# The second gate's weights move behind the first expert's, and the router works on the residual's own sums

## The chip, the cores and the metric

One core of a Trainium2 chip runs the whole kernel. The metric is device time in microseconds (us), as the median over runs. The profile is one further execution of the same program, taken by the hardware profiler.

## The reference, cut to what matters

One transformer block on 256 tokens of width 1024, all in 32-bit floats. `cond @ w_ada` gives six rows of 1024: a shift, a scale and a gate for the mixer, and the same three for the expert layer. The mixer's output `y` enters a residual, which is normalised; the router then picks 4 of 32 experts for each token.

```
shift1, scale1, gate1, shift2, scale2, gate2 = split(cond @ w_ada + b_ada)
y = hybrid_mixer(x * (1 + scale1) + shift1)        # attention, gated linear attention, pooling, @ w_out
x = layer_norm(ALPHA * x + (1 + gate1) * y)
h = x * (1 + scale2) + shift2
logits = h @ w_router + b_router                   # top 4 of 32 for each token, softmax over the 4
y = sum over a token's experts of gate * (clamped_swiglu(h @ w_gate_up[e] + b) @ w_down[e] + b_down[e])
x = layer_norm(ALPHA * x + (1 + gate2) * y)
```

The weights of the 32 experts are read once each: 8 MB for `w_gate_up[e]` and 4 MB for `w_down[e]`.

## The kernel before, in words

The tokens are two tiles of 128 (`t` = 0, 1), the width is eight columns of 128 (`k` = 0 to 7). Work runs in two stages: the block up to the routing, and the expert loop.

**The weight ring.** Nearly all weights pass through tiles of 2 MB (tag `w`, `ring_tile`, line 122), filled by DMAs issued on SyncE's queue (SP) in one fixed order. In the first stage five slots exist (`NA`). The expert stage opens a second pool of three (`NB`), in the memory of the first stage's `early` pool; from there on eight slots are used in turn, five loads into the first pool and three into the second. A load is issued when its slot is free, and SP stands still on a load whose slot is not. The order before: input projection, shift and scale columns, `w_out` (`wo`), the router's weights (`wr`), the gate of the mixer (`ada_g1`, two tiles), the gate of the experts (`ada_g2`, two tiles), then the jobs of the experts: four tiles `g0_0` to `g0_3` (the first expert's gate and up weights), four of expert 1, two of expert 0's down weights, and so on (lines 758 and after).

**The first stage's end.** After the attention, VectorE (DVE) sums the two gates over eight products of a tile row with `cond` (lines 620 to 624): `acc` for the first gate, which TensorE (PE) adds up over partitions into `g1p`, and `g2p` for the second. PE multiplies with `wo` (`py`). For each `t`, DVE forms the residual in place (lines 661, 662: `yg`, `y`), its statistics, and the normalised `n1`. PE turns `n1` (`ph`), DVE and ACT apply `hA` and `hB` column by column into `h2T` (lines 680, 682), PE multiplies with the router's weights (`plg`), a bias is added (`lgp`) and PE turns the result back into rows (`plt`, `lg`). Top 4, one-hots, and a count of earlier tokens follow (`top`, `oh`, `msel`, `ppos`, `posm`): `posm` is the place of a token among its expert's rows.

**The expert loop.** Experts go in pairs. `dispatch` (line 776) makes one-hot rows `pp` from `posm` and gathers the pair's tokens by matmuls of `n1` with `pp` (`pxg`), then applies `hA` and `hB` (`xg`). `gate_up` multiplies `xg` with four tiles of weights, so that a quarter of it frees one slot; `down` follows one expert later. Ahead of pair 6 a branch for overfull experts stands (`more_slots`), with a barrier; until there SP may load only the eight tiles behind the pair's end.

The order on each engine is not the program's: the framework lays it out when the program is built, by priority (earlier in the program first) and by its own model of durations. In the run, each engine follows that order.

Of the kernel before, what the change touches and what calls it, by code (L numbers as in the profile page):

```python
# [9 lines left out]
F32 = mybir.dt.float32  # L10
# [4 lines left out]
OP = mybir.AluOpType  # L15
# [97 lines left out]
def block_kernel(ctx: ExitStack, tc, x, w_ada, w_in, gla_w_a2, pool_w, w_out, w_router, w_gate_up, b_gate_up,  # L113
# [48 lines left out]

    half = const.tile([P, 8], F32, name="half")
# [7 lines left out]
    def layer_norm_stats(st, pool, name):  # L171
        mv = pool.tile([P, 2], F32, tag=f"mv{name}", name=f"mv{name}")
        V.bn_aggr(mv, st.rearrange("p a b -> p (a b)"))
        rs = pool.tile([P, 1], F32, tag=f"rs{name}", name=f"rs{name}")
        rsqrt(rs, mv[:, 1:2], 1.0, LN_EPS, 1, pool, f"rt{name}")
        return mv[:, 0:1], rs


    with tc.tile_pool(name="early", bufs=1) as ea, tc.tile_pool(name="late", bufs=1, side="right") as la_, \
# [30 lines left out]
        def load_cols(j, nm):  # L210
            ts = []
            for i in range(2):
                t = ring_tile(f"{nm}_{i}").rearrange("p (k n) -> p k n", n=D)
                SY.dma_start(t, w_ada[0, i * 512:(i + 1) * 512, j * D:(j + 1) * D].rearrange("(k p) n -> p k n", p=P))
                ts.append(t)
            return ts
# [35 lines left out]
        wr = la_.tile([P, KT, NE], F32, name="wr")  # L252

# [10 lines left out]
        ada_m.append(load_cols(4, "adam1"))  # L264
        wo = {}
# [103 lines left out]
        z2 = la_.tile([P, TT, ZN - O_GV], F32, name="z2")  # L369
# [10 lines left out]
        z_gv = z2[:, :, 0:GVW]  # L380
        z_gr = z2[:, :, GVW:]
# [16 lines left out]
        def second_part(n):  # L398

            c0, c1 = ((W1, W2), (W2, C_GA))[n]  # L400
            for t in range(TT):
                b = bank(f"pz2{t}{n}", "z")
                for k in range(KT):
                    mm(b[:, :c1 - c0], hT[:, k, t * P:(t + 1) * P], wz2[n][:, k], k == 0, k == KT - 1)
                if n == 0:
                    o = C_GV - W1
                    V.tensor_add(z1[:, t, O_GA - o:O_GA], b[:, :o], zb[:, O_GA - o:O_GA])
                    V.tensor_add(z2[:, t, 0:GVW], b[:, o:c1 - c0], zb[:, O_GV:O_GR])
                else:
                    V.tensor_add(z2[:, t, GVW:], b[:, :c1 - c0], zb[:, O_GR:ZN])  # L410
# [3 lines left out]
        gaT = ea.tile([RANK, S], F32, name="gaT")  # L414
# [127 lines left out]
        for j in range(2):  # L542
            acc = la_.tile([P, D], F32, tag=("acc", "g1p")[j], name=f"accm{j}")
            A.mul(acc, ada_m[j][0][:, 0], cond[:, 0:1])
            for k in range(1, KT):
                V.scalar_tensor_tensor(acc, ada_m[j][k // 4][:, k % 4], cond[:, k:k + 1], acc, op0=OP.mult, op1=OP.add)
# [45 lines left out]
        o_gla = la_.tile([P, TT, GVW], F32, name="o_gla")  # L592
# [26 lines left out]

        g1p = la_.tile([P, D], F32, tag="g1p", name="g1p")  # L620
        for ts, acc in ((ada_g1, la_.tile([P, D], F32, tag="acc", name="acc1")), (ada_g2, g2p)):
            V.tensor_scalar(acc, ts[0][:, 0], cond[:, 0:1], None, op0=OP.mult)
            for k in range(1, KT):
                V.scalar_tensor_tensor(acc, ts[k // 4][:, k % 4], cond[:, k:k + 1], acc, op0=OP.mult, op1=OP.add)
            if acc is not g2p:
                for n in range(2):
                    b = bank(f"pg1{n}")
                    mm(b, ones, acc[:, n * 512:(n + 1) * 512], True, False)
                    add_row(b, R_G1 + n, 512, False)
                    V.tensor_scalar(g1p[:, n * 512:(n + 1) * 512], b, 1.0, None, op0=OP.add)  # L630
# [13 lines left out]
        lgp = la_.tile([P, S], F32, tag="qin", name="lgp")  # L644
# [8 lines left out]
        oh = []  # L653
        for t in range(TT):
# [12 lines left out]
            A.activation(n1[:, t, 0:512], xs[:, t, 0:512], AF.Identity, bias=nmr, scale=rs)  # L667
# [3 lines left out]
            for q in range(2):  # L671
                b = bank(f"ph{t}{q}").rearrange("p (j s) -> p j s", j=4)
                for j in range(4):
                    k = 4 * q + j
                    T.transpose(b[:, j], twos(n1[:, t], k), ident)
                for j in range(4):
                    k = 4 * q + j
                    o = h2T[:, k, t * P:(t + 1) * P]
                    if j % 2:
                        A.activation(o, b[:, j], AF.Identity, bias=hB[:, k:k + 1], scale=hA[:, k:k + 1])  # L680
                    else:
                        V.tensor_scalar(o, b[:, j], hA[:, k:k + 1], hB[:, k:k + 1], op0=OP.mult, op1=OP.add)
            b = bank(f"plg{t}")
            for k in range(KT):
                g = slice(32 * (k // 2), 32 * (k // 2) + 32)
                mm(b[g, :P], wr[:, k], h2T[:, k, t * P:(t + 1) * P], k % 2 == 0, k % 2 == 1)
            V.tensor_scalar(lgp[:, t * P:(t + 1) * P], b[:, :P], colv[:, 80:81], None, op0=OP.add)
            b = bank(f"plt{t}")
            mm(b[:, 0:NE], lgp[:, t * P:(t + 1) * P], kc[:, K_I4:K_I4 + NE], True, True)
            V.tensor_copy(lg[:, t], b[:, 0:NE])  # L690
# [11 lines left out]
            V.scalar_tensor_tensor(posm[:, t], b[:, 0:NE], 1.0, msel[:, t], op0=OP.add, op1=OP.mult)  # L702

# [71 lines left out]

    def dispatch(pcol, gcol, nm):
# [3 lines left out]
        for t in range(TT):  # L780
            V.tensor_tensor(pp[:, t], pcol[:, t, :, None].to_broadcast([P, 2, CAP]),
                            iota1[:, None, :].to_broadcast([P, 2, CAP]), op=OP.is_equal)
        xg = wk.tile([P, KT, P], F32, tag="xg", name=f"xg{nm}")
        bs = [mps.tile([P, 4, P], F32, tag="m", name=f"pxg{nm}_{q}") for q in range(2)]
        for t in range(TT):
            for k in range(KT):
                mm(bs[k // 4][:, k % 4], twos(n1[:, t], k), pp[:, t].rearrange("p a s -> p (a s)"),
                   t == 0 and k % 4 == 0, t == TT - 1)
        for k in range(KT):
            if k % 2:  # L790
                A.activation(xg[:, k], bs[k // 4][:, k % 4], AF.Identity, bias=hB[:, k:k + 1], scale=hA[:, k:k + 1])  # L791
            else:
                V.tensor_scalar(xg[:, k], bs[k // 4][:, k % 4], hA[:, k:k + 1], hB[:, k:k + 1], op0=OP.mult, op1=OP.add)  # L793
# [157 lines left out]
    for e in range(NE):  # L951
        i, m = divmod(e, 2)
        if m == 0:
            if i == PAIR_MORE:
                finish_down()
                while done[0] < 12 * i + NA + NB:
                    load_next()
# [8 lines left out]
        if e == 0:  # L966
            last_scale()
            V.tensor_mul(bdn, bdn, g2p[0:NE])
# [59 lines left out]
    r = [wk.tile([P, D], F32, tag="xg", name=f"r{t}") for t in range(TT)]  # L1028
# [42 lines left out]
```

## Time and profile before

| | |
|---|---|
| median of 3 runs | 1128.66 us (1127.93 to 1134.68) |
| profiled execution | 1129.8 us, span 1128.0 us |
| PE busy | 1035.4 us, 92% of the span |
| DVE busy | 318.7 us, 28% |
| bytes moved | 449.49 MB, 398 GB/s over the span |
| DMA queue of SP | 95.7% of 16 engines' span |

The span is the profiled execution's own; 1.8 us lie around it. The granted clock of TensorE is told as a share of full speed: 1.00 is 2.4 GHz, 0.50 is 1.2 GHz. A busy share is an average over stages: the gaps that matter are found by looking at stretches of the span.

### The profile page before, as it was taken

To read this page: it belongs to the slowest core of one execution; us is meant where nothing else is said; L and a number is where in the kernel's file an instruction comes from. 1 tells how busy PE (TensorE), PEld (TensorE's weight loads), DVE (VectorE), ACT (ScalarE), POOL (GpSimd) and SP (SyncE) were. 2 spreads that over 40 slices of the span, in tenths; PEclk is the share of its full clock that TensorE was granted. 3 is DMA by queue.
4 is the path that set the end of the run, shared out by engine and by line. 5 is a ranking of instruction groups with operands and counts; after the bars stand their busy time and mean duration, and the time that the engine had idled before them with its cause. 6 is when DMAs were issued, how large, how long until landed. Compare 5 with 4: busy or idle time off the path is not lost.

```text
span 1128.0 us, 11046 instructions
## 1 busy us (share of the span) xinstructions
PE 1035.4 (92%) x4734; PEld 436.9 (39%) x4735; DVE 318.7 (28%) x587; ACT 98.8 (9%) x205; POOL 41.5 (4%) x43
## 2 busy tenths in 40 slices
PE   6999998999999999996999999989989898989795
PEld 3656545434333333333344343423333333333231
DVE  1459694322222122211122221213221121211113
ACT  1024112100000000000000000000000000000100
POOL 2270000000000000000000000000000000000000
PEclk9999897999999999998999999999999999999998
DMA  9997499999999999999899999999999999999992
GB/s 324 348 385 283 181 378 373 428 423 428 428 428 427 428 428 428 428 427 423 344 427 428 428 428 426 428 427 428 428 428 427 428 429 427 428 427 428 428 414 92
DMA packets 52998, 449.49 MB, mean 398 GB/s; under 512 B 5056, under 2 KB 18768, under 8 KB 28496
## 3 DMA queue, kind: packets, MB, share of 16 engines
q1 hardware_dynamic: 52320, 447.90, 95.7%
q8 instruction: 39, 0.64, 0.2%
q10 hardware_dynamic: 624, 0.83, 0.2%
q14 instruction: 15, 0.12, 0.0%
HBM read 447.67 MB, written 1.05 MB: 398 GB/s over the span
## 4 chain that ended last, share of the span: by engine, by line
PE 29%; DMA 22%; DVE 1%; issue 1%; ACT 0%; POOL 0%; DVEq 0%; POOLq 0%
DMA d<-in_w_down 22%; PE gu L134 13%; PE py L134 7%; PE pxg L134 4%; PE ya L134 3%; PE pyl L134 1%; PE paT L837 1%; DVE yb L855 0%; DVE aT L839 0%; DVE res L919 0%; ACT n L931 0%; PE pln L134 0%; DVE r L1038 0%; DVE yl L1015 0%; DVE st L1019 0%
## 5 line engine op out<-in xcount | busy, mean ns | idle before, releaser
L134 PE MATMUL gu<-g,xg 128*64 128x512 f32 x2048 | 462.5, 595 | 14.0 <-DMA g<-in_w_gate_up 12.6
L134 PEld LDWEIGHTS gu<-g,xg 128*64 128x64 f32 x2048 | 143.2, 137 | 295.5 <-issue 261.0
L134 PE MATMUL py<-d,aT 128*64 128x512 f32 x992 | 227.1, 600 | 13.8 <-DMA d<-in_w_down 12.5
L825 DVE TENSOR_SCALAR g<-gu 128x512 f32<-128x512 f32 x32 | 22.1, 692 | 410.1 <-PE gu L134 410.1
L134 PEld LDWEIGHTS py<-d,aT 128*64 128x64 f32 x992 | 70.0, 137 | 150.5 <-issue 140.8
L134 PE MATMUL pxg<-pp,n 128*128 128x128 f32 x512 | 77.0, 302 | 14.9 <-DVE aT L839 7.0
L134 PEld LDWEIGHTS pxg<-pp,n 128*128 128x128 f32 x512 | 69.2, 208 | 43.0 <-issue 29.6
L855 DVE TENSOR_TENSOR yb<-py,g2p 64x512 f32<-64x512 f32 x60 | 41.3, 689 | 139.0 <-PE py L134 138.4
L134 PE MATMUL ya<-yb,sg_None 128*128 128x512 f32 x120 | 58.2, 607 | 4.9 <-DVE yb L855 4.8
L829 ACT ACTIVATE s<-g 128x512 f32<-128x512 f32 x32 | 20.2, 630 | 464.4 <-DVE g L825 464.4
L793 DVE TENSOR_SCALAR xg<-pxg,hA,hB 128x128 f32<-128x128 f32 x64 | 25.8, 409 | 99.2 <-PE pxg L134 90.0
L791 ACT ACTIVATE xg<-pxg,hB,hA 128x128 f32<-128x128 f32 x64 | 28.7, 457 | 274.3 <-DVE xg L793 273.6
L134 PE MATMUL pz<-wz,hT 128*128 128x512 f32 (+2 forms) x128 | 52.4, 547 | 0.0
L169 POOL TENSOR_TENSOR rsb<-rtb,half 128x2 f32<-128x2 f32 x1 | 0.7, 701 | 950.9 <-DVE rtb L168 950.9
L839 DVE COPY aT<-paT 128x512 f32<-128x512 f32 x32 | 22.1, 692 | 43.9 <-PE paT L837 43.8
L134 PE MATMUL py<-wo,oT 128*128 128x512 f32 x64 | 30.9, 629 | 0.2 <-ACT oT L642 0.2
L134 PEld LDWEIGHTS ya<-yb,sg_None 128*128 128x128 f32 x120 | 20.4, 189 | 26.9 <-issue 17.4
L134 PEld LDWEIGHTS pz<-wz,hT 128*128 128x128 f32 x128 | 23.4, 190 | 17.3 <-issue 14.3
L837 PEld LDWEIGHTS paT<-kc,l 128*128 128x128 f32 x128 | 18.0, 209 | 25.3 <-DVE l L831 15.4
L837 PE MATMUL paT<-kc,l 128*128 128x128 f32 x128 | 23.7, 308 | 0.0
L831 DVE TENSOR_TENSOR l<-l,s 128x512 f32<-128x512 f32 x32 | 22.1, 691 | 3.4 <-DVE l L830 0.5
L134 PE MATMUL pqk<-hT,wz 128*128 128x256 f32 x96 | 22.2, 381 | 0.7 <-DVE hT L332 0.7
(245 smaller groups left out, 519.1 us busy)
## 6 DMA issues: line engine op xcount, KB each, us to landing
g<-in_w_gate_up SPq DMA_DIRECT2D x128, 2048.0 KB, 30.4
d<-in_w_down SPq DMA_DIRECT2D x62, 2048.0 KB, 30.4
adam<-in_w_ada SPq DMA_DIRECT2D x4, 2048.0 KB, 16.7
adag<-in_w_ada SPq DMA_DIRECT2D x4, 2048.0 KB, 9.0
ada<-in_w_ada SPq DMA_DIRECT2D x6, 1024.0 KB, 11.1
wz<-in_w_in SPq DMA_DIRECT2D x8, 760.0 KB, 9.5
wo<-in_w_out SPq DMA_DIRECT2D x2, 1536.0 KB, 10.0
ada<-in_w_ada SPq DMA_DIRECT2D x4, 512.0 KB, 7.4
```

The source lines that it names most:

```text
L134: T.matmul(o, l, r, start=start, stop=stop, skip_group_check=True, **kw)
L169: G.tensor_tensor(o, t[:, :n], half[:, :n], op=OP.pow)
L791: A.activation(xg[:, k], bs[k // 4][:, k % 4], AF.Identity, bias=hB[:, k:k + 1], scale=hA[:, k:k + 1])
L793: V.tensor_scalar(xg[:, k], bs[k // 4][:, k % 4], hA[:, k:k + 1], hB[:, k:k + 1], op0=OP.mult, op1=OP.add)
L825: V.tensor_scalar(g, gu[:, 0], LIMIT, None, op0=OP.min)
L829: A.activation(s, g, AF.Sigmoid, scale=SW_ALPHA)
L831: V.tensor_mul(l, l, s)
L837: T.transpose(b[:, j], act[:, j::4], ident)
L839: V.tensor_copy(aT, b)
L855: V.tensor_mul(yb[m * CAP:(m + 1) * CAP, n * 512:(n + 1) * 512], b[r], g2p[r, n * 512:(n + 1) * 512])
```

## The change

Four things are done, and the tiles are laid out anew to make room.

1. The two tiles of the second gate (`adag2`) leave the first stage. They become jobs 4 and 5 of the expert stage, behind `g0_0` to `g0_3`; DVE sums them after the first expert's `gate_up`, and `last_scale` goes to expert 1. The ring's turn is shifted: of eight loads, numbers 3, 4 and 5 now go to the second pool, so `g0_3` and the two `adag2` tiles lie there.
2. The first gate's tiles are loaded ahead of `wo`, `wr` behind the small constants, and the first gate's sum stands ahead of the linear attention's output.
3. The router works on the residual's sums: `wr2` is the router's weights times `hA` (and times `hB`), their column sums give two rows `rrow` (made behind the attention), and the logits are `rs * (y @ wr2) + rs*(-mu) * row 0 + row 1`. So PE turns `y` itself, as each half is ready, and ACT copies four columns at once.
4. The first pair's tokens are gathered in the routing loop, one `t` at a time, into a tile `xgA` of the outer pool (`gathered`, `modulated`), with its one-hots in `g2p`'s memory. `xgA` then serves the even pairs, one tile of the inner pool the odd.

```
-            i = int(turn[0] % (NA + NB) >= NA)
+            i = int(3 <= turn[0] % (NA + NB) < 3 + NB)
...
+    def one_hot(pp, pcol, t):
+        V.tensor_tensor(pp[:, t], pcol[:, t, :, None].to_broadcast([P, 2, CAP]),
+                        iota1[:, None, :].to_broadcast([P, 2, CAP]), op=OP.is_equal)
+    def gathered(bs, pp, t):
+        for k in range(KT):
+            mm(bs[k // 4][:, k % 4], twos(n1[:, t], k), pp[:, t].rearrange("p a s -> p (a s)"),
+               t == 0 and k % 4 == 0, t == TT - 1)
+    def modulated(xg, bs):
+        for k in range(KT):
+            if k % 2:
+                A.activation(xg[:, k], bs[k // 4][:, k % 4], AF.Identity, bias=hB[:, k:k + 1], scale=hA[:, k:k + 1])
+            else:
+                V.tensor_scalar(xg[:, k], bs[k // 4][:, k % 4], hA[:, k:k + 1], hB[:, k:k + 1], op0=OP.mult, op1=OP.add)
+    def summed(acc, ts):
+        A.mul(acc, ts[0], cond[:, 0:1])
+        for k in range(1, KT):
+            V.scalar_tensor_tensor(acc, ts[k], cond[:, k:k + 1], acc, op0=OP.mult, op1=OP.add)
...
         ada_m.append(load_cols(4, "adam1"))
+        ada_g1 = load_cols(2, "adag1")
         wo = {}
...
-        SY.dma_start(wr.rearrange("p (i k) n -> p i k n", k=2), w_router[0].rearrange("(i p k) n -> p i k n", p=P, k=2))
-        ada_g1 = load_cols(2, "adag1")
-        ada_g2 = load_cols(5, "adag2")
...
+        acc1 = la_.tile([P, D], F32, tag="acc", name="acc1")
+        summed(acc1, ada_g1)
...
+        wr2 = la_.tile([P, 2, KT, NE], F32, tag="qin", name="wr2")
+        for j, h in enumerate((hA, hB)):
+            V.tensor_mul(wr2[:, j], wr, h[:, :, None].to_broadcast([P, KT, NE]))
+        wrs = la_.tile([P, 2, NE], F32, name="wrs")
+        V.tensor_reduce(wrs, wr2.rearrange("p j k e -> p j e k"), axis=AX.X, op=OP.add)
+        b = bank("prow")
+        mm(b[:, 0:2 * NE], ones, wrs.rearrange("p j e -> p (j e)"), True, False)
+        mm(b[:, NE:2 * NE], colv[:, 80:81].to_broadcast([P, P]), kc[:, K_I4:K_I4 + NE], False, True)
+        rrow = la_.tile([P, 2, NE], F32, name="rrow")
+        V.tensor_copy(rrow, b[:, 0:2 * NE].rearrange("p (j e) -> p j e", j=2))
...
                 V.bn_stats(st6[:, n], y)
+                b = bank(f"ph{t}{n}").rearrange("p (j s) -> p j s", j=4)
+                for j in range(4):
+                    T.transpose(b[:, j], twos(xs[:, t], 4 * n + j), ident)
+                A.copy(h2T[:, 4 * n:4 * n + 4, t * P:(t + 1) * P], b)
...
+            row = la_.tile([P, NE], F32, tag="row", name=f"row{t}")
+            V.scalar_tensor_tensor(row, rrow[:, 0], nmr, rrow[:, 1], op0=OP.mult, op1=OP.add)
+            b = bank(f"plg{t}")
+            for k in range(KT):
+                mm(b[:, 0:NE], h2T[:, k, t * P:(t + 1) * P], wr2[:, 0, k], k == 0, k == KT - 1)
+            V.scalar_tensor_tensor(lg[:, t], b[:, 0:NE], rs, row, op0=OP.mult, op1=OP.add)
...
             V.scalar_tensor_tensor(posm[:, t], b[:, 0:NE], 1.0, msel[:, t], op0=OP.add, op1=OP.mult)
+            one_hot(ppA, posm[:, :, 0:2], t)
+            if t == 0:
+                first = [bank(f"pxgA{q}", "z").rearrange("p (j s) -> p j s", j=4) for q in range(2)]
+            gathered(first, ppA, t)
+        modulated(xgA, first)
...
+        if e == 0:
+            jobs += [("gate", 0, lambda e, i: load_columns(5, i, f"adag2_{i}"), (0, i)) for i in range(2)]
...
-                while done[0] < 12 * i + NA + NB:
+                while done[0] < 12 * i + 2 + NA + NB:
...
         if e == 0:
+            summed(g2p, weights("gate", 0))
+        elif e == 1:
             last_scale()
```

## Rows read from the trace of the kernel before

**Rows 1.** The page: rate in 40 slices; SP's queue; the chain's lines.

```profile
GB/s 324 348 385 283 181 378 373 428 423 428 428 428 427 428 428 428 428 427 423 344 427 428 428 428 426 428 427 428 428 428 427 428 429 427 428 427 428 428 414 92
...
q1 hardware_dynamic: 52320, 447.90, 95.7%
...
DMA d<-in_w_down 22%; PE gu L134 13%; PE py L134 7%; PE pxg L134 4%; PE ya L134 3%; PE pyl L134 1%; PE paT L837 1%; DVE yb L855 0%; DVE aT L839 0%; DVE res L919 0%; ACT n L931 0%; PE pln L134 0%; DVE r L1038 0%; DVE yl L1015 0%; DVE st L1019 0%
```

**Rows 2.** Stretches: length, busy by engine, then PE's clock, DMA share, GB/s.

```profile
126.00:141.00 15.00, 14.97 (x75) 8.91 (x75) 9.47 (x15) 0.98 (x2) 2.66 (x2) 0.96 0.01 4
147.00:186.00 39.00, 33.43 (x132) 20.01 (x132) 30.72 (x78) 8.09 (x17) 1.10 (x2) 0.82 0.98 399
186.00:191.00 5.00, 5.00 (x29) 2.44 (x30) 1.95 (x6) 3.00 (x5) 0.00 (x0) 1.00 0.70 290
191.00:200.00 9.00, 9.00 (x46) 3.10 (x44) 0.00 (x0) 0.00 (x0) 0.00 (x0) 1.00 0.91 353
200.00:505.00 305.00, 294.99 (x1382) 113.94 (x1378) 67.67 (x118) 18.83 (x38) 0.00 (x0) 1.00 1.01 427
...
580.00:1000.00 420.00, 389.73 (x1822) 148.75 (x1818) 89.35 (x163) 24.50 (x50) 0.00 (x0) 1.00 1.01 427
```

**Rows 3.** Timeline of SP's queue: start, length, line, operation, count.

```profile
117.98 0.37 SPq L214 DMA_DIRECT2D adag<-in_w_ada  x1
140.13 0.37 SPq L214 DMA_DIRECT2D adag<-in_w_ada  x1
147.09 0.34 SPq L737 DMA_DIRECT2D g<-in_w_gate_up  x1
164.54 1.03 SPq L737 DMA_DIRECT2D g<-in_w_gate_up  x2
190.91 3.76 SPq L742 DMA_DIRECT2D d<-in_w_down  x2
```

**Rows 4.** Waits of SP's queue in its first 200 us: total, times, longest.

```profile
SPq L742 <- PE gu L134: 27.3, 2, 24.3
```

**Rows 5.** Timeline of PE: start, length, line, operation, output and inputs.

```profile
119.09 2.48 PE L134 MATMUL pcol<-kc,accm 128*128 128x4 f32 x16
...
153.94 10.57 PE L134 MATMUL py<-wo,oT 128*128 128x512 f32 x24 [0.24 <-ACT oT L642]
165.17 1.22 PE L675 MATMUL ph<-kc,n 128*128 128x128 f32 x8 [0.67 <-ACT n L667]
...
181.59 5.69 PE L134 MATMUL pxg<-pp,n 128*128 128x128 f32 x32
...
187.21 7.09 PE L134 MATMUL gu<-g,xg 128*64 128x512 f32 x32
...
220.10 4.04 PE L134 MATMUL pxg<-pp,n 128*128 128x128 f32 x32
```

**Rows 6.** Timeline of DVE and ACT: sums, linear attention's state, residual, routing, one copy.

```profile
116.68 1.28 DVE L546 SCALAR_TENSOR_TENSOR accm<-adam,cond,accm 128x1024 f32<-128x1024 f32 x1
124.47 0.36 DVE L588 COPY sts<-kv 128x192 f32<-128x192 f32 x1 [1.32 <-PE kv L134]
164.64 0.68 DVE L661 TENSOR_TENSOR yg<-py,g1p 128x512 f32<-128x512 f32 x1
165.36 0.69 DVE L662 SCALAR_TENSOR_TENSOR n<-n,yg 128x512 f32<-128x512 f32 x1
178.24 0.19 DVE L690 COPY lg<-plt 128x32 f32<-128x32 f32 x1 [0.73 <-PE plt L134]
180.62 0.19 DVE L702 SCALAR_TENSOR_TENSOR posm<-ppos,msel 128x32 f32<-128x32 f32 x1 [0.26 <-PE ppos L134]
202.38 0.63 ACT L829 ACTIVATE s<-g 128x512 f32<-128x512 f32 x1 [11.91 <-DVE g L825]
```

**Rows 7.** Timeline around the barrier: PE's last down product, SP's next load.

```profile
510.29 3.65 PE L134 MATMUL py<-d,aT 128*64 128x512 f32 x16 [1.16 <-DMA d<-in_w_down]
550.65 0.82 SPq L742 DMA_DIRECT2D d<-in_w_down  x2
```

More of the change, by code (lines that the diff above doesn't have):

```diff
@@ L161, in add_row @@
         mm(o, sel[:, r:r + 1].to_broadcast([96, P]), row3[:, :n], start, True)
+    xgA = const.tile([P, KT, P], F32, name="xgA")
     half = const.tile([P, 8], F32, name="half")
@@ L176, in layer_norm_stats, with load_columns @@
         return mv[:, 0:1], rs
+    def one_hot(pp, pcol, t):
[15 more added lines that the diff above has]
+            V.scalar_tensor_tensor(acc, ts[k], cond[:, k:k + 1], acc, op0=OP.mult, op1=OP.add)
+    def load_columns(j, i, name):
+        t = ring_tile(name).rearrange("p (k n) -> p k n", n=D)
+        SY.dma_start(t, w_ada[0, i * 512:(i + 1) * 512, j * D:(j + 1) * D].rearrange("(k p) n -> p k n", p=P))
+        return [t[:, k] for k in range(4)]
     with tc.tile_pool(name="early", bufs=1) as ea, tc.tile_pool(name="late", bufs=1, side="right") as la_, \
@@ L210, in load_cols @@
         def load_cols(j, nm):
[L211 to L216, printed above, removed]
+            return load_columns(j, 0, f"{nm}_0") + load_columns(j, 1, f"{nm}_1")
         first_ada = load_ada1(0)
@@ L368, in block_kernel @@
         z1 = ea.tile([P, TT, O_GV], F32, name="z1")
-        z2 = la_.tile([P, TT, ZN - O_GV], F32, name="z2")
+        z_gv = la_.tile([P, TT, GVW], F32, name="z_gv")
+        z_gr = la_.tile([P, TT, GVW], F32, tag="gr", name="z_gr")
         a = W1 - C_FV
@@ L407, in second_part @@
                     V.tensor_add(z1[:, t, O_GA - o:O_GA], b[:, :o], zb[:, O_GA - o:O_GA])
-                    V.tensor_add(z2[:, t, 0:GVW], b[:, o:c1 - c0], zb[:, O_GV:O_GR])
+                    V.tensor_add(z_gv[:, t], b[:, o:c1 - c0], zb[:, O_GV:O_GR])
                 else:
-                    V.tensor_add(z2[:, t, GVW:], b[:, :c1 - c0], zb[:, O_GR:ZN])
+                    V.tensor_add(z_gr[:, t], b[:, :c1 - c0], zb[:, O_GR:ZN])
         lin = ea.tile([P, TT, FH + GKW], F32, name="lin")
-        gaT = ea.tile([RANK, S], F32, name="gaT")
+        gaT = ea.tile([P, 2, S], F32, tag="pm", name="gaT")[0:RANK, 0]
         b = bank("gaT")
@@ L543, in block_kernel @@
             acc = la_.tile([P, D], F32, tag=("acc", "g1p")[j], name=f"accm{j}")
-            A.mul(acc, ada_m[j][0][:, 0], cond[:, 0:1])
-            for k in range(1, KT):
-                V.scalar_tensor_tensor(acc, ada_m[j][k // 4][:, k % 4], cond[:, k:k + 1], acc, op0=OP.mult, op1=OP.add)
+            summed(acc, ada_m[j])
             b = bank(f"pcol{j}", "z")[:, 0:32].rearrange("p (q m) -> p q m", q=8)
@@ L591, in block_kernel @@
                                            op0=OP.mult, op1=OP.add)
-        o_gla = la_.tile([P, TT, GVW], F32, name="o_gla")
+        acc1 = la_.tile([P, D], F32, tag="acc", name="acc1")
+        summed(acc1, ada_g1)
+        o_gla = la_.tile([P, TT, GVW], F32, tag="gr", name="o_gla")
         for t in range(TT):
@@ L617, in block_kernel @@
             V.tensor_mul(o_gla[:, t], o_gla[:, t], sg[:, t])
-        g1p = la_.tile([P, D], F32, tag="g1p", name="g1p")
[L621 to L630, printed above, removed]
+        wr2 = la_.tile([P, 2, KT, NE], F32, tag="qin", name="wr2")
[8 more added lines that the diff above has]
+        V.tensor_copy(rrow, b[:, 0:2 * NE].rearrange("p (j e) -> p j e", j=2))
+        g1p = la_.tile([P, D], F32, tag="g1p", name="g1p")
+        for n in range(2):
+            b = bank(f"pg1{n}")
+            mm(b, ones, acc1[:, n * 512:(n + 1) * 512], True, False)
+            add_row(b, R_G1 + n, 512, False)
+            V.tensor_scalar(g1p[:, n * 512:(n + 1) * 512], b, 1.0, None, op0=OP.add)
         py = [[bank(f"py{t}{n}", "z") for n in range(2)] for t in (1, 0)][::-1]
@@ L653, in block_kernel @@
         oh = []
+        ppA = g2p[:, 0:TT * P].rearrange("p (t m s) -> p t m s", t=TT, m=2)
         for t in range(TT):
@@ L774, in weights @@
         return loaded.pop((kind, e))
+    evens = [str(i) for i in range(0, NE // 2, 2)]
     def dispatch(pcol, gcol, nm):
@@ L780, in dispatch @@
         for t in range(TT):
[L781 to L793, printed above, removed]
+            one_hot(pp, pcol, t)
+        if nm == "0":
+            xg = xgA
+        else:
+            xg = xgA if nm in evens else wk.tile([P, KT, P], F32, tag="xg", name=f"xg{nm}", bufs=1)
+            bs = [mps.tile([P, 4, P], F32, tag="m", name=f"pxg{nm}_{q}") for q in range(2)]
+            for t in range(TT):
+                gathered(bs, pp, t)
+            modulated(xg, bs)
         def gates(m=None):
@@ L1027, in block_kernel @@
     stats = [(mv[:, t, 0:1], rs[:, t:t + 1]) for t in range(TT)]
-    r = [wk.tile([P, D], F32, tag="xg", name=f"r{t}") for t in range(TT)]
+    r = [xgA.rearrange("p k s -> p (k s)"), wk.tile([P, D], F32, tag="xg", name="r1", bufs=1)]
     for t in range(TT):
```

24 lines of the change are left out of this document (1 added, 23 removed).

## The prediction

> **What bounds the kernel now.** I read the page's rate by slices first, then its chain, then stretches, then SP's queue. The rate stands at 427 to 428 GB/s in nearly every slice from the eighth on, and the chain that ends last is mostly DMA of down weights [rows 1]: the expert loop is bound by the stream of weights. From 200 to 505 us and from 580 to 1000 us the stream runs at 427 GB/s without a hole [rows 2]. So the kernel ends a fixed time after the stream starts for good, and only holes in the stream, or bytes still to come, can move it.
>
> The reader should see the holes before 200 us. From 126 to 141 us nothing flows (4 GB/s), though PE is busy throughout [rows 2]: SP stands at the fourth gate tile until 140.13, because its slot is freed only when DVE has half summed the first gate [rows 3]. After that everything goes out that eight slots can hold: `g0` and `g1`, the last of them just behind 164.54 [rows 3]. SP then waits up to 24.3 us for `gu`, PE's first expert product [rows 4]: all eight slots are full, and nothing can be loaded until a quarter of `gu` has been computed. `gu` starts at 187.21 [rows 5], the next load goes out at 190.91 [rows 3], 3.7 us later. The stream sags to 290 GB/s from 186 to 191 and recovers [rows 2]. **That instant, 190.91, is what counts**: the hole at 126 costs nothing by itself, as slots are full well before.
>
> **The balance of the change.** Before, when the slots are full they hold eight tiles of experts 0 and 1, and the second gate is already used up. After, they hold `g0`, the two gate tiles and only two tiles of expert 1. So when the stream starts for good, two more tiles of 2 MB (2.097 million bytes) are still to come: at 427 GB/s [rows 2] 4.91 us each, **9.8 us lost**. What is gained is how much sooner `gu` starts. Break-even is `gu` at 187.21 - 9.8 = 177.4.
>
> A rule bears on this price. The Trainium skill (DMA: Bandwidth & Descriptors, Where 436 GB/s comes from) says that the memory side, about 358 GB/s for a core, binds such loads. By that the two tiles would cost 11.7 us (an estimate) and the sum would come out 1.9 us later; the trace's 427 GB/s disagrees, and decides.
>
> **When `gu` starts, step by step.**
>
> *Up to the last `py`.* PE is busy nearly without a break from 126 (14.97 of 15 us to 141 [rows 2]) to 164.5, where the last `py` ends (153.94 + 10.57) [rows 5], so taking 20 us of gate sums off DVE doesn't end it sooner: the gate's rows for PE (`pg`) only move forward among the same work. What is put in front of it now: the residual's transposes, 12 of 16 ahead of the last half (8 took 1.22 us [rows 5], so 1.8); logits of `t` = 0, 16 passes at the pace of the small products that also load 128 columns each (2.48/16 = 0.155 [rows 5]; 1.9 to 2.5, I take 1.9, since those ran with stalls); the two row products, 0.4. The last `py` ends at 164.5 + 4.1 = **168.6**. Lower bound 164.5 if all of it falls into gaps; upper 171.5 if sums of the first gate, 1.28 us each [rows 6], get in front of links of the linear attention's state on DVE, of which the row at 124.47 is one [rows 6]: two or three such collisions, 2.6 to 3.8 us, that PE's other work can't hide.
>
> *Residual to logits.* `yg` and `y` take 164.5 to 166.05 before [rows 6]: 1.55 us, so 170.15. Behind it four transposes (0.6), ACT's copy of 128x512, priced by another ACT pass of that size (0.63 [rows 6]; from PSUM rather than SBUF, so 0.5 to 0.9), the last eight passes of the logits (1.0), `lg` (0.2), and 0.3 of handovers: 2.7. In PE's order the gather of `t` = 0 may stand in front of these transposes; I count 0.7 of its 2 to 2.85 us. `lg` ends at **173.6**. The statistics run beside: five small operations after `y`, at the 0.2 to 0.7 of such rows [rows 6], so 1 to 3.5 us, and 3.2 are there.
>
> *Logits to place.* From `lg`'s end (178.43) to `posm`'s (180.81) it is 2.4 us [rows 6], and nothing in it changes: 176.0. One-hot 0.3: 176.3.
>
> *Gather of `t` = 1.* Half of `pxg`. The whole took 5.69 us here and 4.04 us at 220 [rows 5]; halves 2.85 and 2.0. The clock granted is 0.82 over 147 to 186 and 1.00 at 200 to 505 [rows 2]; I take 2.4. **`gu` starts at 178.7**, since its first columns of `xg` are ready before the gather ends. The Trainium skill (TensorE: Matmul & The Clock Gate, Part 1) has the clock low by default and released by activity. By that the fuller PE queue favours 2.0, and the sum would be 0.4 us less; the rows at both levels agree in sense.
>
> *First load and end.* 178.7 + 3.7 = 182.4. Against 190.91 that is 8.5 us gained; less 9.8: **1.3 us later**.
>
> **Edits at nothing.** The first gate's loads take `wo`'s early slots and `wo` theirs; the same bytes flow, and SP is at the loads behind them by 117.98 [rows 3], with `py` starting behind `pcol`, which ends at 121.6 [rows 5]. If a part of `wo` came late, PE would wait for one tile of the stream, up to 4.9 us; the 3.6 us between the two rows cover most of it. `wr` goes ahead of the second part's weights; it is 0.13 MB, 0.3 us at 427 GB/s, and that is its cost if a stage waits for them. The two `adag2` tiles and `g1_0`, `g1_1` queue on SP behind slots of the second pool, free when the linear attention's output is done, ahead of the `py` row at 153.94 [rows 5]; `wo`'s second slot comes free last, at 168.6, and one tile of 4.9 us is in before 182. Without that cover: second rival. The second gate's sum (one ACT pass, seven of 1.28 us) runs on DVE while PE does two halves of `gu` of 7.09 us [rows 5], and its slots come back before the stream needs them. `last_scale` moves by one expert and stays ahead of the first `down`. In the loop the alternating `xg` tiles are two as before. At the barrier PE waits 1.16 us for the last down tile [rows 7], so the data already set that point; the hole before 550.65 [rows 7] stays.
>
> The profiled execution was 1129.8 us, 1.1 above the median of 1128.66. So 1131.1 by its count, 1130.0 by the median's.
>
> **Rivals.**
>
> *Routing shortens in full* (faster, but little). All small work hides, `py` ends at 164.5, nothing stands in front of the transposes: `gu` at 173.5, 5.2 us earlier: 1125. For it: DVE is nearly free of sums from 130 on. Against: PE follows an order laid out before the run, and earlier work has priority over the last `py`.
>
> *Slots of the second pool come late* (slower). The new layout puts `adag2` into memory that a tile of the routing holds to its end, about 176. SP, in order, stands in front of four tiles, 19.6 us of stream, which then start at 176 and make expert loads follow at 195.6, where break-even is 181.1: 14.5 later, 1143. It decides as soon as that slot is freed after 161.5. Against: before, the three loads of that pool left right behind 164.54, long ahead of `posm` [rows 3, 6].
>
> *Routing doesn't get shorter.* PE's order puts work of `t` = 0 that waits on DVE ahead of `t` = 1, and `gu` stays between 183 and 187: 1134.5 to 1138.5. For it: PE's queue already stood waiting in this stretch, 5.6 us idle of 39 [rows 2].
>
> *The filled hole pays by itself.* If more slots than eight took part, or the stream never stopped, some 15 us of 126 to 141 would come back: 1115. Against: SP's 24.3 us wait [rows 4].
>
> **How the numbers follow.** Forecast 0.55 (1127 to 1133.5), full shortening 0.18, no shortening 0.16, late slots 0.06, filled hole 0.05. The range 1124 to 1138 holds the first three; own range of the likeliest 1127 to 1133.5. A measurement tells about 1%, 11.3 us, from no change: faster by that only in the last case, slower in the late slots and a tail of no shortening. Faster 0.05, same 0.87, slower 0.08.
>
> **What would show it.** SP: `g0` issued from about 118 on, no hole of 15 us, then a longer one before the restart; restart near 182. PE: `gu` at 177 to 181, the last `py` at 167 to 170. Stream 427 GB/s from there. I am wrong if `gu` starts before 172 or after 187, if the restart doesn't follow `gu` by 3.7 us, or if the time doesn't move by restart plus 9.8.

## The result: 8.4 us slower, and the profile after

The changed kernel takes 1136.68 us (median of 12 runs, 1133.29 to 1139.76) against 1128.30 for the kernel before on the same chip (12 runs, 1126.05 to 1134.68): ratio 1.0058, 95% interval 1.0039 to 1.0077. That is slower beyond its interval, though inside the 1% called "no change" beforehand. The time lies in the stated range of 1124 to 1138, but the likeliest case said 1130 (1127 to 1133.5) and was missed. What came are the numbers of the third rival, "routing doesn't get shorter": `gu` between 183 and 187, 1134.5 to 1138.5. Its reason holds only in part, as the step by step account shows.

The page of the kernel after: rate in 40 slices, chain by line. They answer to [rows 1].

```profile
GB/s 319 351 380 257 279 370 186 430 427 427 429 427 426 429 427 427 427 428 425 353 428 430 427 426 428 427 429 427 428 429 426 427 429 426 427 429 427 427 416 108
...
DMA d<-in_w_down 22%; PE gu L134 9%; PE py L134 6%; DMA g<-in_w_gate_up 4%; PE ya L134 3%; PE pxg L134 3%; PE pyl L134 1%; PE paT L865 1%; DVE aT L867 0%; DVE yb L883 0%; DVE res L947 0%; DVE yl L1045 0%; DVE xgA L1068 0%; DVE st L1049 0%; DVE xgA L1062 0%
```

The bound is the same: from the eighth slice on the stream runs at 425 to 430 GB/s, but for the same dip in the twentieth and the last two slices. So the difference has to lie ahead of that. The fifth slice rose from 181 to 279, the seventh fell from 373 to 186.

Stretches of the kernel after, columns as in [rows 2]: length, busy time by engine, then PE's clock, DMA share, GB/s.

```profile
126.00:141.00 15.00, 15.00 (x51) 8.65 (x52) 10.53 (x17) 0.49 (x1) 1.03 (x1) 0.78 0.52 196
147.00:186.00 39.00, 36.24 (x153) 22.61 (x154) 20.49 (x66) 7.85 (x15) 2.04 (x3) 0.93 0.72 289
186.00:191.00 5.00, 5.00 (x24) 1.61 (x22) 5.00 (x10) 1.68 (x4) 0.00 (x0) 0.89 0.12 26
200.00:505.00 305.00, 289.29 (x1348) 113.45 (x1346) 66.31 (x116) 20.12 (x39) 0.00 (x0) 1.00 1.01 428
```

The hole of 126 to 141 is half filled (196 GB/s, 4 before), as the change says. A longer one has opened: 289 instead of 399 GB/s from 147 to 186, and 26 instead of 290 from 186 to 191.

SP's queue in the kernel after, against [rows 3]:

```profile
121.28 0.34 SPq L765 DMA_DIRECT2D g<-in_w_gate_up  x1
131.66 0.33 SPq L765 DMA_DIRECT2D g<-in_w_gate_up  x1
141.68 0.81 SPq L765 DMA_DIRECT2D g<-in_w_gate_up  x2
149.27 0.93 SPq L207 DMA_DIRECT2D adag<-in_w_ada  x2
156.91 0.34 SPq L765 DMA_DIRECT2D g<-in_w_gate_up  x1
172.10 0.34 SPq L765 DMA_DIRECT2D g<-in_w_gate_up  x1
189.88 3.76 SPq L765 DMA_DIRECT2D g<-in_w_gate_up  x2
```

Eight slots: `g0`, both tiles of the second gate, two tiles of expert 1. Then nothing for 17.8 us until `gu` frees one. The restart is at 189.88, where 190.91 stood before, and two tiles more are still to come.

PE from the last product of the output weights to `gu`, against [rows 5], then DVE's logits and places against [rows 6]:

```profile
169.25 2.82 PE L134 MATMUL py<-wo,oT 128*128 128x512 f32 x6
...
173.67 0.48 PE L699 MATMUL ph<-kc,n 128*128 128x128 f32 x2 [0.48 <-DVE n L695]
173.98 2.05 PE L134 MATMUL pxgA<-g2p,n 128*128 128x128 f32 x16
175.87 0.39 PE L699 MATMUL ph<-kc,n 128*128 128x128 f32 x2
...
177.35 1.06 PE L134 MATMUL plg<-wr,h2T 128*128 128x32 f32 x8
...
180.22 0.57 PE L134 MATMUL ppos<-msel,kc 128*128 128x32 f32 x2 [1.70 <-DVE msel L720]
...
181.56 3.78 PE L134 MATMUL pxgA<-g2p,n 128*128 128x128 f32 x16
185.27 8.00 PE L134 MATMUL gu<-g,xgA 128*64 128x512 f32 x32
```

```profile
178.45 0.25 DVE L709 SCALAR_TENSOR_TENSOR lg<-plg,rsa,row 128x32 f32<-128x32 f32 x1 [1.61 <-PE plg L134]
180.83 0.19 DVE L725 SCALAR_TENSOR_TENSOR posm<-ppos,msel 128x32 f32<-128x32 f32 x1 [0.20 <-PE ppos L134]
```

What to see: the gather of `t` = 0 (173.98) splits the four transposes on which the logits of `t` = 1 hang (173.67 and 175.87). After the logits PE stands 1.70 us, and the gather of `t` = 1 then takes 3.78 us where the 16 passes for `t` = 0 took 2.05, 7.6 us before.

### The profile page after: what moved, and what is told of

The parts are those of the page before. It is cut to its first block, busy times and chain, and to the rows that moved or that the text cites. A ratio compares the mean times of both kernels' runs of the same rounds, so it can differ in the third digit from the quotient of the medians.

```text
span 1134.9 us, 11054 instructions
## 1 busy us (share of the span) xinstructions
PE 1034.9 (91%) x4734; PEld 441.1 (39%) x4735; DVE 314.3 (28%) x583; ACT 99.7 (9%) x203; POOL 39.4 (3%) x43
## 5 line engine op out<-in xcount | busy, mean ns | idle before, releaser
L134 PE MATMUL gu<-g,xgA 128*64 128x512 f32 x1024 | 232.7, 597 | 9.9 <-DMA g<-in_w_gate_up 7.7
L134 PE MATMUL gu<-g,xg 128*64 128x512 f32 x1024 | 232.8, 596 | 8.8 <-DMA g<-in_w_gate_up 8.8
L134 PEld LDWEIGHTS py<-d,aT 128*64 128x64 f32 x992 | 72.3, 137 | 151.9 <-issue 138.9
L134 PEld LDWEIGHTS gu<-g,xgA 128*64 128x64 f32 x1024 | 72.2, 137 | 151.0 <-issue 131.2
L134 PEld LDWEIGHTS gu<-g,xg 128*64 128x64 f32 x1024 | 71.6, 136 | 150.7 <-issue 128.9
L134 PE MATMUL pxg<-pp,n 128*128 128x128 f32 x480 | 69.5, 293 | 15.0 <-DVE aT L867 7.1
L134 PEld LDWEIGHTS pxg<-pp,n 128*128 128x128 f32 x480 | 62.4, 200 | 42.2 <-issue 28.7
L134 PE MATMUL pqk<-hT,wz 128*128 128x256 f32 x96 | 24.9, 414 | 0.7 <-DVE hT L358 0.7
L194 ACT ACTIVATE xgA<-pxg,hB,hA 128x128 f32<-128x128 f32 x28 | 12.6, 457 | 146.0 <-DVE xgA L196 145.7
L196 DVE TENSOR_SCALAR xg<-pxg,hA,hB 128x128 f32<-128x128 f32 x32 | 12.9, 409 | 45.0 <-PE pxg L134 40.1
## 6 DMA issues: line engine op xcount, KB each, us to landing
adag<-in_w_ada SPq DMA_DIRECT2D x4, 2048.0 KB, 11.7
wz<-in_w_in SPq DMA_DIRECT2D x8, 760.0 KB, 10.1
```

What stands on the lines that cost most here:

```text
L134: T.matmul(o, l, r, start=start, stop=stop, skip_group_check=True, **kw)
```

## The experiments

The sum under test is the prediction's (theory A, wherever a run's theory A speaks of the restart): the span is the stream's restart, plus 4.9 us for each tile that then is more to come, plus a constant. Here it is for every profiled execution (us). "Lands" is the time from the issue of the restart's load until its data have landed; "rest" is the span less restart and tiles.

```
kernel                          restart  lands  tiles more   span    rest
before                          190.91    7.6       0       1128.0   937.1
after                           189.88    7.8       2       1134.9   935.2
after, profiled again (e10)     191.38    7.8       2       1137.7   936.5
e1 gate in the first stage      189.55    9.8       0       1125.3   935.8
e2 only the gate moved          193.81    7.7       1       1134.9   936.2
e3 gate not loaded              188.01    7.7       0       1125.2   937.2
e4 gather of t = 0 later        185.81    7.7       2       1132.1   936.5
e6 first gate's sum later       191.38    7.8       2       1137.4   936.2
e5 = e1 + e4                    185.76   12.6       0       1126.6   940.8
e7 = e5 + e6                    186.48   11.7       0       1124.6   938.1
e8 = e5, other slots first      183.53    7.7       0       1118.6   935.1
e9 = e7, other slots first      185.82   10.0       0       1123.5   937.7
```

The kernel before ran beside each group: 1128.96 us with e1 to e4 (32 runs, 1125.41 to 1135.63), 1127.98 with e5 to e7 (24 runs), 1130.10 with e8 to e10 (23 runs).

**e1: the second gate back in the first stage.** The new router, the early gather and the shifted ring stay; the early gather's one-hots get other memory. `last_scale` goes back to expert 0 with the sum, against what was written beforehand, so e1 alone doesn't separate the tiles from it; e3 does.

```diff
+        ada_g2 = load_cols(5, "adag2")        # behind wo
 ...
+        summed(g2p, ada_g2)                   # ahead of py
 ...
-            jobs += [("gate", 0, ..., (0, i)) for i in range(2)]
 ...
-            summed(g2p, weights("gate", 0))
```

> Keeps the new router and the first pair's early gather; loads the second gate's two tiles in the first stage again (behind wo) and sums them there; the one-hots of the first gather get other memory. Theory A (the stream of weights ends a fixed time after its restart behind the first quarter of gu, plus 4.9 us for each 2 MB tile then still to come): gu starts between 183 and 187, restart 3.7 to 4.6 us later, two tiles fewer to come than in the changed kernel, so about 9.8 us below its 1136.7: 1125 to 1129, at or a little below the kernel before. Theory B (the changed kernel loses by its new order in the expert stage, the sum beside gu, the tile xgA, the later last_scale and the shifted ring, not by the two tiles): since all of these but the sum stay, it remains above 1133.

Measured: 1126.81 us (12 runs), ratio 0.9971 (0.9951 to 0.9991).

```profile
189.55 3.76 SPq L773 DMA_DIRECT2D d<-in_w_down  x2
```

`gu` starts at 185.76 and the restart is where the kernel after has it, but no tile is missing. Each against the kernel before on its own chip, e1 is 0.87% below the kernel after (0.9971 and 1.0058), 9.8 us, and two tiles are 9.8 us. The loss is the second gate's place in the expert stage, not the new routing.

**e2: only the second gate moved, the rest as before** (the shifted ring and the later `last_scale` go with it).

```diff
-        ada_g2 = load_cols(5, "adag2")
 ...
+            jobs += [("gate", 0, lambda e, i: load_columns(5, i, f"adag2_{i}"), (0, i)) for i in range(2)]
 ...
+            summed(g2p, weights("gate", 0))   # behind the first gate_up
```

> The kernel before with the second gate's two tiles alone moved behind the first expert's four, with the shifted ring; router, first gate and first gather as before. Theory A: gu at 186 to 188, restart about 190.5, two more tiles: 1137 to 1139.5, 9 to 11 us slower than before. Theory B: this part is free or a gain, as it frees DVE and fills the hole at 126 us: 1126 to 1130.

Measured: 1138.61 us (9 runs), ratio 1.0086 (1.0056 to 1.0116). DVE and SP in that kernel:

```profile
181.61 1.27 DVE L173 SCALAR_TENSOR_TENSOR g2p<-adag,cond,g2p 128x1024 f32<-128x1024 f32 x1
182.80 0.18 DVE L713 SCALAR_TENSOR_TENSOR posm<-ppos,msel 128x32 f32<-128x32 f32 x1
```

```profile
176.89 0.33 SPq L753 DMA_DIRECT2D d<-in_w_down  x1
193.81 3.76 SPq L748 DMA_DIRECT2D g<-in_w_gate_up  x2
```

Here the gate's tiles arrive early enough for DVE to sum them between 171.9 and 182.9, in the middle of the routing: seven links of 1.27 us, `posm` at 182.80, `gu` at 190.12, 2.9 us later than before. One slot does come free early (176.89), so only one tile more is to come. The part alone is at least as slow as the whole change: its ratio is the highest of all, but its interval overlaps the one of the kernel after, so whether the rest of the change bought something back isn't shown.

**e3: the kernel after without the second gate's load and sum** (`g2p` is a constant; that part is left out).

```diff
-            jobs += [("gate", 0, ..., (0, i)) for i in range(2)]
 ...
-            summed(g2p, weights("gate", 0))
+            V.memset(g2p, 0.01)
```

> The changed kernel without the second gate's load and sum: its two tiles are not loaded and its row is a constant (that part of the computation is left out); four tiles of expert 1 fill the ring. Theory A: 9.8 us below the changed kernel, and 0.9 us more because the sum no longer stands on DVE and ACT between the columns of xgA: 1125 to 1128. Theory B: the order of the expert stage stays, so it gives back the sum's 1 us at most: above 1134.

Measured: 1126.65 us (12 runs), ratio 0.9961 (0.9939 to 0.9983).

```profile
179.64 3.78 PE L134 MATMUL pxgA<-g2p,n 128*128 128x128 f32 x16
183.35 8.04 PE L134 MATMUL gu<-g,xgA 128*64 128x512 f32 x32
```

Leaving out the gate's bytes and slots gains 10.9 us (0.97%) on the kernel after, with `last_scale`, `xgA` and the shifted ring as they are there: theory B falls. Two tiles are 9.8; in the profiled executions the restart is also 1.9 us sooner, which the first stage brings (its first products ran at full pace, see e10). The gate's sum isn't what slows the first half of `gu`: without it the half takes 8.04 us as well.

**e4: the gather of `t` = 0 emitted behind the logits of `t` = 1.** Theory: the 2 us gather stands in PE's way.

```diff
-            gathered(first, ppA, t)
+        gathered(first, ppA, 1)
 ...                                         # behind the logits' passes:
+            if t:
+                gathered(first, ppA, 0)
```

> The changed kernel with the gather of t = 0 put behind the logits of t = 1 in the program. In the changed kernel PE's order has it (2.05 us at 173.98) ahead of the last two transposes of t = 1. Theory A with PE's order as a cause of the late gu: the logits of t = 1 end about 1.5 us sooner, gu starts at 183.5 to 184.5, the time falls by 1 to 1.5 us: about 1135.4. Rival (the clock and the gather's own 3.8 us set the end, the gather merely moves): no change within 0.7 us, or 1 us slower.

Measured: 1133.35 us (12 runs), ratio 1.0028 (1.0006 to 1.0050): 0.30% or 3.4 us less than after, where 1 to 1.5 were expected; with an interval of about 0.29% either way that is just clear of noise. PE, then the stretch from 180 to 186 of this kernel and of the kernel after:

```profile
176.82 1.66 PE L134 MATMUL pxgA<-g2p,n 128*128 128x128 f32 x12
...
180.07 2.12 PE L134 MATMUL pxgA<-g2p,n 128*128 128x128 f32 x16
182.12 7.09 PE L134 MATMUL gu<-g,xgA 128*64 128x512 f32 x32
```

```profile
180.00:186.00 6.00, 6.00 (x35) 3.31 (x36) 5.70 (x18) 2.76 (x5) 0.00 (x0) 1.00 0.02 8
```

```profile
180.00:186.00 6.00, 5.64 (x23) 4.75 (x25) 3.90 (x17) 1.08 (x2) 0.00 (x0) 0.53 0.08 26
```

The last products end 0.4 us later than in the kernel after (172.48), and yet `gu` starts 3.15 us sooner. About half is the order. The other half, 1.66 us in the last gather, is the clock, granted at 1.00 (2.4 GHz) instead of 0.53 on average, mostly its lower level of 1.2 GHz: the gather now fills the gap in which PE stood for the places. Over all profiled executions with the new routing this splits cleanly. Five have the old order and a wait of 1.70 us, and their last gather takes 3.40 to 3.78 us (after twice, e1, e3, e6). Five have the new order (e4, e5, e7, e8, e9), and it takes 2.12 us in each. The Trainium skill (TensorE: Matmul & The Clock Gate, Part 1) has the clock low by default and released by activity; the traces agree in sense, 3.40 to 3.78 us behind the wait and 2.12 without it. Order and wait change together in all ten, so which of them the clock follows isn't separated. The kernel before, with the old routing, shows it too: PE waits 1.74 us up to 172.13, and the granted clock is 0.50 from 172 to 185.

**e5: e1 and e4 together.**

> The kernel of e1 (second gate back in the first stage) with the edit of e4: the gather of t = 0 emitted behind the logits of t = 1. Theory A: the end is the stream's restart plus 936 us (935 to 937 in six kernels so far) and the gather's place works alike whether the second gate lies in the slots or not. In e4 it brought `gu` from 185.27 to 182.12 and the restart 4.1 us forward; so here the restart goes from 189.55 to about 186, the span from 1125.3 to about 1122, the time from 1126.8 to 1123 to 1124. Theory B: e1's order of the first stage differs, the gather of t = 0 does not stand in front of the transposes of t = 1 there or the clock stays low in spite of it: 1126 to 1127.5.

Measured: 1127.24 us (12 runs), ratio 0.9986 (0.9967 to 1.0006). Not what theory A said. The restart came at 185.76 as expected, and the span didn't follow: 940.8 us. The time is theory B's, its reasons aren't: the gather did move, the clock was full, and `gu` started at 182.07. SP and three stretches of e5, then the restart's load (size, us from issue to landing) in e5 and in e1:

```profile
142.06 0.34 SPq L770 DMA_DIRECT2D g<-in_w_gate_up  x1
154.62 18.18 SPq L770 DMA_DIRECT2D g<-in_w_gate_up  x7
185.76 3.76 SPq L775 DMA_DIRECT2D d<-in_w_down  x2
```

```profile
147.00:155.00 8.00, 8.00 (x24) 3.73 (x23) 6.70 (x11) 0.00 (x0) 1.01 (x1) 1.00 0.22 94
180.00:186.00 6.00, 6.00 (x37) 3.31 (x38) 3.94 (x16) 2.17 (x5) 0.00 (x0) 1.00 1.02 414
186.00:191.00 5.00, 5.00 (x28) 1.79 (x26) 0.00 (x0) 0.84 (x1) 0.00 (x0) 1.00 0.99 370
```

```profile
d<-in_w_down SPq DMA_DIRECT2D x1, 2048.0 KB, 12.6
d<-in_w_down SPq DMA_DIRECT2D x1, 2048.0 KB, 9.8
```

From 180 on the stream is busy: the restart comes while tiles asked for earlier still flow. From 154.62 on seven tiles go out before the restart, 7 times 4.9 is 34.4 us, so they flow until about 189 (an estimate), and a load issued at 185.76 only joins their queue: it lands 12.6 us later, where it takes 7.6 to 7.8 us in the eight executions whose stream had run dry, or all but dry. The theory needs a second half: the end follows the **later** of two instants, the first slot freed by `gu` and the landing of what is already asked for. With the 4.9 us that the load came late taken off, e5's rest is 935.9. In e1 the landing was already the later one, by about 2 us (9.8 for 7.7), which a rest of 935.8 didn't show. Corrected in this way all twelve rests lie within 933.7 to 937.2; why e1 and e7 are lowest (933.7 and 934.1) stays open.

**e6: the kernel after with the first gate's sum emitted where it was.**

```diff
-        acc1 = ...; summed(acc1, ada_g1)      # ahead of o_gla
 ...
+        acc1 = ...; summed(acc1, ada_g1)      # behind rrow, ahead of g1p
```

> The changed kernel with the first gate's sum emitted again where it was before the change, behind the linear attention and ahead of its rows for PE. Theory A: in the changed kernel the sum's seven links of 1.28 us on DVE stand in front of the modulation's sums and of the linear attention's state (the columns' product is done at 122.4 instead of 119.1, a state's link waits at 126), and that delays the last `py`; with the sum later the columns' product is back near 119, the last `py` ends about 3 us sooner, at 168 to 170, and the restart goes from 189.9 to about 187: 1133 to 1134. Theory B: PE's own work between 126 and 172 sets the end of `py`: the last `py` stays at 171.5 to 172.5 and the time at 1136 to 1137. Theory C: the later sum holds the first gate's slots longer or collides with the routing of t = 0, and the last `py` comes later than 173: over 1138.

Measured: 1136.97 us (7 runs), ratio 1.0070 (1.0045 to 1.0095): no gain. The time is theory B's; the profiled execution, near the upper end of its runs at 1139.11, has the last `py` end at 175.04, as late as the unaltered kernel's in e10 (174.98). It doesn't settle theory A, for DVE's compiled order put the sum's first link into the same place all the same:

```profile
114.31 1.28 DVE L202 SCALAR_TENSOR_TENSOR accm<-adam,cond,accm 128x1024 f32<-128x1024 f32 x1
115.50 1.28 DVE L202 SCALAR_TENSOR_TENSOR acc<-adag,cond,acc 128x1024 f32<-128x1024 f32 x1
116.69 1.28 DVE L202 SCALAR_TENSOR_TENSOR accm<-adam,cond,accm 128x1024 f32<-128x1024 f32 x1
```

**e7: e5 and e6 together.** Both diffs, on e1.

> The kernel of e1 with both edits: the gather of t = 0 behind the logits of t = 1, and the first gate's sum behind the linear attention. Theory A: both gains add, the restart comes at 183 to 185 and the time is 1120 to 1122, the fastest here. Theory B: only the gather's place counts: as the run of e1 with the gather alone, 1123 to 1124. Theory C: with two gates to sum on DVE between the linear attention and the last `py`, the sums (16 links of 1.28 us, 20 us) end later than the attention does and hold up the residual: slower than e1, over 1127.

Measured: 1126.41 us (12 runs), ratio 0.9972 (0.9951 to 0.9994). Theory A's 1120 to 1122 fell; the 1123 to 1124 of B, which rested on the same half theory, and C's "over 1127" too. The stream is at 423 GB/s from 180 to 186 here as well, the restart's load lands 11.7 us after its issue, and the rest is 938.1.

**e8: e5 with the second pool's slots taken first.** A test of the theory's second half. In e5 SP stands from 142.06 to 154.62 at a slot that waits for the second gate's sum, with free slots behind it.

```diff
-            i = int(3 <= turn[0] % (NA + NB) < 3 + NB)
+            i = int(1 <= turn[0] % (NA + NB) < 1 + NB)
```

> The kernel of e5 with one number changed: the second pool's three slots are taken by the second to fourth expert tile instead of the fourth to sixth. Reason to try it: in e5 the restart came at 185.76 and yet the span was 1126.6, 940.8 us later instead of 936. Theory A: restart plus 936 us holds only while the stream has run dry by then. In e5 it had not (390 GB/s from 183 to 186, 431 from 189): what bounds it is the older hole, 94 GB/s from 147 to 155, where SP stands 12.2 us at a slot that the second gate's sum frees at 154.6, with slots of the second pool free behind it. Taking those first lets two tiles go out near 149.5 and fills most of the hole; the eight slots are then full about 5 us sooner, the stream is dry near 183, and the restart at 185.8 counts again: span near 1122, time 1123 to 1124.5. Theory B: the lost 4.9 us of e5 have another place (the loop or the second routing near 513): 1126.5 to 1127.5, as e5. Theory C: the second pool's slots are in fact freed later than 154: slower than e5, over 1129.

Measured: 1124.00 us (12 runs, 1120.44 to 1126.58), ratio 0.9944 (0.9924 to 0.9964), faster than both kernels.

```profile
139.82 0.82 SPq L770 DMA_DIRECT2D g<-in_w_gate_up  x2
147.43 10.53 SPq L770 DMA_DIRECT2D g<-in_w_gate_up  x5
...
183.53 3.76 SPq L775 DMA_DIRECT2D d<-in_w_down  x2
```

```profile
147.00:155.00 8.00, 8.00 (x21) 3.57 (x20) 7.86 (x9) 0.00 (x0) 0.00 (x0) 1.00 1.00 426
180.00:186.00 6.00, 6.00 (x30) 2.00 (x30) 3.01 (x13) 2.55 (x4) 0.00 (x0) 1.00 0.50 143
```

The hole of 147 to 155 is gone (426 GB/s, 94 in e5), the stream runs dry ahead of the restart (143 from 180 to 186), and the rest is 935.1 again. The restart's load lands at 191.27 instead of 198.34, 7.1 us sooner. Of that 2.2 us are a sooner restart, which comes from the first stage, where this edit changes nothing (e8's first products ran at full pace, see e10), so some 4.8 are the edit's. Against the kernel before e8 is 0.42% below e5, 4.7 us (0.28% either way). The profiled execution is the fastest of the twelve, so the 8 us between the two spans overstate it.

**e9: e7 with the same number changed.**

> The kernel of e7 with the same number changed. Theory A: as in e8, a gain of 2 to 3 us on e7's 1126.4: e7's hole from 147 to 155 is smaller (262 GB/s), but 0 GB/s from 131 to 136 and 111 from 141 to 147 stay: 1123.5 to 1125. Theory B: no gain, 1126 to 1127.

Measured: 1124.58 us (12 runs), ratio 0.9952 (0.9932 to 0.9972). That lies in theory A's range, but 0.20% below e7 with an interval of about 0.29% either way is no gain clear of noise. Nor is the reason A's: the restart's load lands 10.0 us after its issue, so the older loads still hold it. The first gate's sum adds nothing that shows to e8.

**e10: the kernel after, profiled again.**

> The changed kernel unaltered, a second look. In its first look the early products ran at half pace (12 passes in 5.49 us at 13.69, 2.86 in e1 to e4) and PE's last product of the output weights ended at 172.07. Theory A: that is a chance of the execution; if this one has 2.86 there, the columns' product comes 2 to 3 us sooner, the last product ends at 169.5 to 172.5 (sooner only if no other stretch at half clock takes its place, as in e4 at 110 to 126), and `gu` starts at 182.5 to 185.5. Theory B: it belongs to the changed code: 5.49 again, 172 and 185.3.

Measured once: 1139.49 us. The first products of e10 and of e8, then the last `py` and `gu` of e10:

```profile
14.05 5.49 PE L134 MATMUL pqk<-hT,wz 128*128 128x256 f32 x12 [0.71 <-DVE hT L358]
```

```profile
13.37 2.86 PE L134 MATMUL pqk<-hT,wz 128*128 128x256 f32 x12 [0.70 <-DVE hT L359]
```

```profile
172.16 2.82 PE L134 MATMUL py<-wo,oT 128*128 128x512 f32 x6
...
187.68 7.09 PE L134 MATMUL gu<-g,xgA 128*64 128x512 f32 x32
```

The first products took 5.49 us again, but theory B's 172 and 185.3 didn't come: the last `py` ends at 174.98 and `gu` starts at 187.68, 2.9 and 2.4 us later in the same kernel. Nor is the slow start the changed code's own. Of the kernels with its first products, e1, e3, e4 and e8 had 2.86 us (so had e2 and the kernel before) and e5, e6, e7 and e9 4.58 to 5.49. What decides stays open. The products that started by 13.4 us ran at full pace, those from 13.7 on did not; but a later start is itself a sign that the work ahead had been slow.

## Where the prediction was right and where it was wrong, step by step

The range of 1124 to 1138 held the time because it took in a rival of chance 0.16; the likeliest case, of chance 0.55, missed it by 3.2 us. A little slower, within the 1%, came as said.

**The balance was right.** Two tiles in the slots were to cost 9.8 us, and e1, which has the same restart without them, is 9.8 us faster than the kernel after (some 3.3 us either way, so the close match is partly chance; e1's load also landed 2 us late). The restart moved by 1.0 us, so 8.8 lost were due, where the spans differ by 6.9 and the medians by 8.4. In the eight executions where the stream was dry at the restart the rests scatter from 935.1 to 937.2, which is how well the sum holds; what the 1.9 us between before and after come from stays open. By the Trainium skill's 358 GB/s (DMA: Bandwidth & Descriptors, Where 436 GB/s comes from) the two tiles would have cost 11.7 us (an estimate). The stream's 427 to 428 GB/s disagrees, and decides; the medians alone don't part 9.8 from 11.7.

**The step that failed is "when `gu` starts": 178.7 said, 185.27 measured.** With the load behind it, the restart came 7.5 us late (189.88 for 182.4). By its terms, with PE's first product of the columns before, after and in e3 for the first of them:

```profile
107.68 1.94 PE L134 MATMUL pcol<-kc,accm 128*128 128x4 f32 x16
110.19 1.94 PE L134 MATMUL pcol<-kc,accm 128*128 128x4 f32 x16
108.27 1.94 PE L134 MATMUL pcol<-kc,accm 128*128 128x4 f32 x16
```

- *Up to the last `py`*: 172.07 for 168.6, 3.5 late, 0.6 beyond the upper bound of 171.5. From the first product of the columns to the end of the last `py` it takes 61.9 us, in e3 as well, against 56.8 before: 5.1 us more, where 4.1 were said. The larger part of the miss is the start of the stretch, which I took as fixed: 2.5 us later in the kernel after, 0.6 in e3, whose first products ran at full pace, and 4.5 in e10. So it varies between executions, and isn't shown to be the change's. Of the 5.1 us, 3.0 lie ahead of the first `py`: a link of the first gate stands between two of the modulation's (as in e6), and two pairs of state products, one of them waiting 1.02 us on DVE, stand in front of `py`, where before the first `py` went ahead of such a pair. That these cause it wasn't shown: the only try, e6, left the link where it was.
- *Residual to logits*: 6.6 us from the end of `py` to `lg` for 5.0. The gather of `t` = 0 stood in front with all its 2.05 us, of which I counted 0.7. Shown by e4, where it is 4.8 us.
- *Logits to place*: 2.3 for 2.4, right. The one-hot behind it: 0.5 for 0.3.
- *Gather of `t` = 1*: 3.78 for 2.4, outside the bounds of 2.0 to 2.85. I took PE's clock from the averages of two stretches of the kernel before (0.82 hides that it was 0.50 from 172 to 185) instead of asking what the new order would leave PE to do. The wait of 1.70 us and the clock of 0.53 came together, and e4 took both away at once.
- *First load*: 4.6 us from `gu` to the restart for 3.7, the same low clock. That the restart would follow by 3.7 was one of the signs named for being wrong. In e3 it is 4.7 without the sum, in e4 and e10 3.7 with it. That the sum of the second gate hides, priced at nothing, was right.

The third rival's reason, work of `t` = 0 ahead of `t` = 1, was the right one for some 3 of the 6.6 us by which `gu` came late (e4). The other 3.5 lie ahead of the last `py`, which that rival doesn't name, and the routing did get shorter: from the end of the last `py` to `gu` it is 13.2 us, against 22.7 before and 10.1 said. That the time fell into that rival's range is therefore partly luck, and in e10 `gu` lies outside it. The rival that shortens in full fell, with `gu` 11.8 us later than it had it. So did the hole that pays by itself: it was half filled, and the kernel got slower.

**The edits at nothing.** `g0` goes out from 121.28 (about 118 said), `adag2` at 149.27, long before `posm`: the rival of late slots fell, as argued. At the barrier nothing new shows: the next load goes out at 558.53, 7.9 us after the 550.65 of before, where the span is 6.9 longer.

**The filled hole.** "The hole at 126 costs nothing by itself" was true of the kernel before and is not a rule. There the slots were all asked for by 166.09, but not full "well before": the last of these loads landed at 191.5, and the restart's load at 198.5, where 196.4 would have been possible (an estimate, one tile of 4.9 us later). With the hole left as it was, a sooner `gu` could have gained some 2 us and no more. e5 to e8 show the hole and the restart as two bounds, the later one counting. In e1 the landing already was the later, so e5, which moves only the restart, gains nothing on it; e8 moves both and is 6.1 us faster than the kernel before by medians. In the kernel after the restart is far behind the landing (26 GB/s from 186 to 191), and there the restart alone counts, as the prediction had it.

## What to carry to other kernels

In a kernel bound by a stream through a ring of slots, count at the moment when the ring is full what still has to come: bytes that go through the ring early for another purpose are paid for there, however empty the hole that they fill. In these runs a hole cost nothing only where the loads asked for had landed before the next slot was freed. So compare when the last load asked for lands with when the consumer frees a slot, and move both. When PE's waits are removed or made, price the products behind them at either clock: here 1.7 us of waiting went with 1.3 to 2.6 more in the products behind it.

## What was not expected of the hardware

The low clock behind a short wait: 16 passes in 2.12 us in each of five kernels, 3.40 to 3.78 in the four others (e4's paragraph). Behind them the first half of `gu` took 8.00 and 8.04 us in two executions, and 7.09 to 7.18 in three as it does at full clock. And the first products after 13 us, 5.49 instead of 2.86 us in some kernels, with a granted clock of 1.00 shown from 10 to 20 us in both cases: there the row's duration tells of the slow pace, the clock's column doesn't. The first product of the columns then starts at 110.2 to 112.3 us instead of 107.5 to 108.3.
